# Weight sums of the first fifteen seven-product projections: from GpSimd to VectorE, in another order

## The chip, the core and the metric

One core of a Trainium2 chip runs the whole program once. The time is the device time of one execution in microseconds. Before the change three executions took 2179.86, 2184.01 and 2181.0 us, a median of 2181.0 us.

## What is computed

The reference is one step of a one-layer encoder over 1024 prompt tokens and 64 sample tokens of width 1024, all in float32. Cut to what this change touches, it is a normalised input times one large weight matrix:

```python
rq, rk, rv, rg, sq, sk, sv, ga, gb = split(rms_norm(x, g_attn) @ w_in)
q, k, v = rope(rq), rope(rk) / 16, rv                  # 4 heads of 256
o, state = retention(q, k, v)                          # chunkwise, chunks of 64
B = sliding_window_attention(sq, sk, sv)               # 16 query heads, 2 key/value heads of 64
```

Gates, output projections, cross-attention and a SwiGLU block follow; nothing of them is changed.

## The kernel before, in words

Activations lie transposed: features on the 128 partitions, the 1088 tokens along the free axis, cut into two halves of 544. Every float32 operand is kept as a rounded high part and a remainder, and each product is three matmuls (high by high, high by low, low by high).

Most projections take 256 output columns at a time and are 2 by 2 block products: two weight rows of blocks by two column halves, times two feature halves by two token halves. `strassen` (L254) computes them with seven products in place of eight, in the order P1, P2, P6, P5, P7, P3, P4. One product is 24 matmuls of 272 columns and fills one PSUM pair of banks; three pairs are in turn. The operands on the activation side (B11, B21, T1 to T4 and so on) are made once. The weight side is made anew for every projection by `weight_ops` (L173): it takes two raw tiles of 128 by 1024, `raws[0]` with the blocks a11 and a12 and `raws[1]` with a21 and a22, and forms P1 = a11, P2 = a12, P4 = a22, P5 = a21 + a22, P6 = a21 + a22 - a11, P7 = a11 - a21, P3 = a12 - P6. The four sums (L190, L191, L193, L196) are done in place by GpSimd. `put` (L181) sends each result through `split` (L122): ScalarE casts the high part into a `wq` tile (L123), VectorE subtracts to get the low part (L124). There are five `wq` tiles in turn and two raw tiles, so a weight is prepared a few products ahead and waits for a tile that TensorE has left.

VectorE also adds partial products (`u` tiles, L259), takes results out of PSUM (`stage`, L598), applies the rotary terms (L629 to L635; for heads 2 and 3 the last two on GpSimd), adds up squares for the norm (`token_squares`, L478) and does a good part of the retention steps (`retention`, from L740): the low halves of `ks`, `qs`, `st` and `ss`, the scaled keys `kt` (L768) and values `vb` (L777), the masked scores `sf` (L789).

`project_phase` (L572) runs these projections in this order: values of head 0 (eight plain products), then with seven products keys 0, queries 0, keys 1, queries 1, values 1, SWA queries 0, the same four for heads 2 and 3, then the keys and values of SWA together (L686): fifteen projections. After them come the last SWA queries and the gates. Retention steps of the heads are woven in between. After the first queries come the root-mean-square factors: `token_roots` (L480) has TensorE add up the squares over partitions (`pt`, L487).

A scheduler lays down one fixed order per engine before the program runs, and each engine then works in that order. So an instruction that moves from GpSimd to VectorE also moves its neighbours, on TensorE too.

Of the kernel before, what the change touches and what calls it, by code (L numbers as in the profile page):

```python
# [109 lines left out]
class Kernel:  # L110
# [62 lines left out]
    def weight_ops(self, raws, n=512, skip=()):  # L173

        nc = self.nc
        half = [[raws[i][:, j * n:(j + 1) * n] for j in range(2)] for i in range(2)]
        (a11, a12), (a21, a22) = half
        add, sub = ALU.add, ALU.subtract
        w = {}

        def put(name, src):  # L181
            if name in skip:
                return
            q = w[name] = self.new_op({"P7": 2, "P6": -1, "P5": -1}.get(name, 0))
            self.split(src, q[:, 0, :n], q[:, 1, :n])

        tt = nc.gpsimd.tensor_tensor
        put("P1", a11)
        put("P2", a12)
        tt(out=a11, in0=a11, in1=a21, op=sub)  # L190
        tt(out=a21, in0=a21, in1=a22, op=add)  # L191
        put("P7", a11)
        tt(out=a11, in0=a22, in1=a11, op=sub)  # L193
        put("P6", a11)
        put("P5", a21)
        tt(out=a12, in0=a12, in1=a11, op=sub)  # L196
        put("P3", a12)
        put("P4", a22)
        return w
# [153 lines left out]
    def run(self):  # L353
        nc, tc, io = self.nc, self.tc, self.io
        with ExitStack() as ctx:
            cp = ctx.enter_context(tc.tile_pool(name="const", bufs=1, reuse_waits="tile"))
            self.np = ctx.enter_context(tc.tile_pool(name="norm", bufs=1, reuse_waits="tile"))
            dp = ctx.enter_context(tc.tile_pool(name="scratch", bufs=1, reuse_waits="tile", space=DRAM))

            self.ident = cp.tile([P, P], F32, name="ident")  # L360
            self.ones = cp.tile([P, P], F32, name="ones")
            self.gains = cp.tile([P, 5, KT], F32, name="gains")
            self.load(self.gains, io["g_all"])
            nc.vector.memset(self.ones, 1.0)
            self.rstd = cp.tile([P, T], F32, name="rstd")
            nc.scalar.mul(self.rstd[:, :1], self.ones[:, :1], 1.0)

            self.root = cp.tile([P, len(CH), 3], F32, name="root")
            self.rtok = cp.tile([P, 9], F32, name="rtok")
            nc.vector.memset(self.rtok, 1.0)  # L370
            self.mtok = cp.tile([P, 2], F32, name="mtok")
            self.tab = cp.tile([P, 2, H, 3], F32, name="tab")
            self.tok = cp.tile([P, 3, H, 9], F32, name="tok")
            self.sinks = cp.tile([P, NPAIR], F32, name="sinks")

            self.d_mk = dp.tile([H, P, 2, NMEM], F32, name="d_mk")
            self.d_mv = dp.tile([H, P, 2, NMEM], F32, name="d_mv")
            self.d_ret = dp.tile([KT, P, T], F32, name="d_ret")
            self.d_swa = dp.tile([KT, P, T], F32, name="d_swa")
            self.d_gate = [dp.tile([KT, P, T], F32, name=f"d_gate{i}") for i in range(3)]  # L380
            self.d_mix = dp.tile([KT, P, T], F32, name="d_mix")
            self.d_h = [dp.tile([KT, P, T], F32, name=f"d_h{i}") for i in range(2)]
            self.d_op = dp.tile([len(OPS), FT // 2, P, HALF], F32, name="d_op")
            self.d_rb = dp.tile([16, 64 * 256], F32, name="d_rb")

            self.d_qkv = dp.tile([3, KT, P, T], F32, name="d_qkv")
            self.d_skv = dp.tile([2, P, T], F32, name="d_skv")
            self.d_sq = dp.tile([NPAIR // 2, P, 17, 2, 64], F32, name="d_sq")

            with ExitStack() as sctx:  # L390
                self.rings = [Ring(sctx.enter_context(tc.tile_pool(name=f"ring{i}", bufs=1, reuse_waits="tile", side="right")))
                              for i in range(2)]
                self.mem = sctx.enter_context(ExitStack())
                self.left = sctx.enter_context(ExitStack())
                self.sixth, self.turns, self.held, self.last_held = None, 0, [], 0
                self.wp = self.left.enter_context(tc.tile_pool(name="weights", bufs=2, reuse_waits="tile"))
                self.project_phase()
                with self.plain_psum(2, side="right"):
                    self.swa_phase()
                with self.plain_psum(side="right"):  # L400
                    self.merge_swa()
                    self.mem.close()
                    self.cross_phase()
                rp = sctx.enter_context(tc.tile_pool(name="rf", bufs=1, reuse_waits="tile", side="right"))
                self.rstd_f = rp.tile([P, T], F32, name="rstd_f")
                self.temp = sctx.enter_context(ExitStack())
                self.new_b12(self.temp, side="right")
                self.cross_out_phase()
                self.ffn_phase()
# [162 lines left out]
    def project_phase(self):  # L572
        nc, tc, io = self.nc, self.tc, self.io
        with ExitStack() as ctx:
# [89 lines left out]
            with ExitStack() as rctx:  # L664
                self.ra = rctx.enter_context(tc.tile_pool(name="ra", bufs=1, reuse_waits="tile"))
                rope = self.ra.tile([P, 2, T], F32, name="rope")
                for t in range(2):
                    self.load(rope[:, :, half(t)], io["c_rope"][:, :, half(t)])
                for h in range(H):
                    rotated(pair("w_k", h) if h else first, h, 1)  # L670
                    if h == 0:
                        self.token_squares()
                    rotated(pair("w_q", h), h, 0)
                    if h == 0:
                        self.token_roots()
                        self.retention_setup()
                    else:
                        values(pair("w_v", h), h)
                    if h:
                        project(pair("w_sq", h - 1), queries(h - 1))  # L680
                    self.retention(h)
                    if h == 0:
                        self.spread_roots()
                    if h == 1:
                        self.later.append(self.bias_table)
                project(self.load_ops((io["w_sk"], io["w_sv"])), lambda i, t, o: self.store(self.d_skv[i, :, half(t)], o))  # L686
            project(pair("w_sq", 3), queries(3))
            steps = [0, 0, 0, 0, 1, 2, 2, 3, 3, 3, 2, 0]
            for idx, w, act in ((1, "w_ga", AF.Sigmoid), (0, "w_rg", AF.Silu), (2, "w_gb", AF.Sigmoid)):
# [1144 lines left out]
```

## Time and profile before

| | |
|---|---|
| Runs, median | 2181.0 us |
| The profiled execution: its time, its span | 2183.19 us, 2181.1 us |
| TensorE matmul busy | 2142.3 us, 98% |
| VectorE busy | 1553.4 us, 71% |
| ScalarE busy | 876.4 us, 40% |
| GpSimd busy | 651.7 us, 30% |
| Mean granted TensorE clock | 0.995 |
| First sum (L190) of the fifteen projections, first sum of the next one | 40.18 us, 462.81 us |

The span goes from the first to the last instruction; 2.1 us of the execution's time lie around it. Matmuls are pipelined, so "busy" says that TensorE has something under way and not that it works at its peak; what stops it is read from the waits. The changed stretch is about 36 to 462 us.

### The profile page before, as it was taken

What the parts mean: (1) busy time and instruction counts of PE and PEld (TensorE: products, weight loads), DVE (VectorE), ACT (ScalarE), POOL (GpSimd) and SP (SyncE); (2) the same over time, 40 slices, a digit from 0 to 9 for tenths busy, and PEclk for the clock granted to TensorE, in tenths of its full rate; (3) what the DMA queues carried; (4) which work ended last, traced back from release to release, by engine and by line L of the source; (5) the groups of instructions that cost most, each with busy time, mean ns of one, the idle gap of its engine ahead of it and who ended that gap; (6) DMA issues with size and microseconds to landing.
All of it is one profiled execution on the core that took longest, in us unless ns stands there. A gap on an engine that the chain in (4) does not pass through costs nothing. (4 is left out here: it accounts for less than half of the span.)

```text
span 2181.1 us, 41848 instructions
## 1 busy us (share of the span) xinstructions
PE 2142.3 (98%) x16389; PEld 2089.0 (96%) x16389; DVE 1553.4 (71%) x2824; ACT 876.4 (40%) x1898; POOL 651.7 (30%) x498
## 2 busy tenths in 40 slices
PE   8999999999999999999999999999999999999997
PEld 8999999999999997889999999999999999999997
DVE  8996868776687658665455555768777777787688
ACT  7344424344344447553233333333322322344343
POOL 1223233342344214430000000014565555514531
PEclk9999999999999999999999999999999999999999
DMA  6434354435344467326443111422333323294433
GB/s 208 154 131 114 114 152 125 137 111 159 103 160 164 166 206 246 118 80 219 124 155 120 40 49 59 146 87 91 121 124 116 105 96 120 94 331 128 135 107 119
DMA packets 181446, 290.84 MB, mean 133 GB/s; under 512 B 40290, under 2 KB 109314, under 8 KB 181250
## 3 DMA queue, kind: packets, MB, share of 16 engines
q1 hardware_dynamic: 176130, 278.18, 40.1%
q10 hardware_dynamic: 4608, 8.36, 1.0%
q8 instruction: 129, 2.11, 0.4%
q0 software_dynamic: 512, 1.64, 0.2%
q14 instruction: 67, 0.55, 0.1%
HBM read 196.95 MB, written 91.16 MB: 132 GB/s over the span
## 5 line engine op out<-in xcount | busy, mean ns | idle before, releaser
L124 DVE TENSOR_TENSOR wq<-raw,wq 128x512 fp32r<-128x512 f32 (+1 forms) x499 | 443.9, 893 | 134.8 <-ACT wq L123 131.4
L123 ACT CAST wq<-raw 128x512 fp32r<-128x512 f32 (+1 forms) x499 | 303.1, 614 | 567.1 <-PE pq L215 223.3
L212 PE MATMUL pq<-T,wq 128*128 128x272 f32 x1832 | 492.0, 288 | 4.9 <-ACT wq L123 3.3
L213 PE MATMUL pq<-T,wq 128*128 128x272 f32 x1832 | 492.9, 289 | 0.0
L213 PE MATMUL pq<-B,wq 128*128 128x272 f32 x1592 | 428.2, 289 | 2.9 <-DVE B L124 2.6
L212 PE MATMUL pq<-B,wq 128*128 128x272 f32 x1592 | 426.6, 288 | 0.5 <-ACT B L123 0.5
L190 POOL TENSOR_TENSOR raw<-raw 128x512 f32<-128x512 f32 (+1 forms) x59 | 86.0, 1458 | 1036.5 <-DVE rs_r L301 483.0
L215 PE MATMUL pq<-T,wq 128*128 128x272 f32 x1832 | 382.8, 289 | 1.5 <-DVE wq L124 1.5
L212 PEld LDWEIGHTS pq<-T,wq 128*128 128x128 f32 x1832 | 345.0, 188 | 6.7 <-ACT wq L123 3.1
L213 PEld LDWEIGHTS pq<-T,wq 128*128 128x128 f32 x1832 | 344.9, 188 | 1.2 <-issue 1.1
L215 PE MATMUL pq<-B,wq 128*128 128x272 f32 x1592 | 332.2, 289 | 0.0
L213 PEld LDWEIGHTS pq<-B,wq 128*128 128x128 f32 x1592 | 299.5, 188 | 4.3 <-DVE B L124 4.2
L212 PEld LDWEIGHTS pq<-B,wq 128*128 128x128 f32 x1592 | 299.4, 188 | 1.4 <-ACT B L123 0.9
L215 PEld LDWEIGHTS pq<-T,wq 128*128 128x128 f32 x1832 | 290.2, 190 | 2.6 <-DVE wq L124 1.8
L215 PEld LDWEIGHTS pq<-B,wq 128*128 128x128 f32 x1592 | 252.2, 190 | 0.5 <-issue 0.4
L259 DVE TENSOR_TENSOR u<-pq,u 128x544 f32<-128x544 f32 x177 | 127.2, 719 | 95.5 <-PE pq L215 95.4
L193 POOL TENSOR_TENSOR raw<-raw 128x512 f32<-128x512 f32 (+1 forms) x59 | 80.8, 1370 | 91.4 <-DVE wq L124 81.5
L598 DVE TENSOR_TENSOR stage<-pq,u 128x544 f32<-128x544 f32 x112 | 80.3, 717 | 36.9 <-PE pq L215 32.4
L191 POOL TENSOR_TENSOR raw<-raw 128x512 f32<-128x512 f32 (+1 forms) x59 | 88.8, 1505 | 3.6
L196 POOL TENSOR_TENSOR raw<-raw 128x512 f32<-128x512 f32 (+1 forms) x59 | 84.0, 1423 | 4.4
L1483 POOL TENSOR_TENSOR stage<-stage,rstd_f 128x544 f32<-128x544 f32 x40 | 63.9, 1607 | 39.1 <-ACT stage L1482 39.1
L156 PE MATMUL pd<-xc,wq 128*128 128x256 f32 (+1 forms) x256 | 74.5, 291 | 0.0
(383 smaller groups left out, 4548.4 us busy)
## 6 DMA issues: line engine op xcount, KB each, us to landing
hl<-d_op SPq DMA_DIRECT2D x85, 272.0 KB, 5.3
d_qkv<-stage SPq DMA_DIRECT2D x44, 272.0 KB, 2.7
d_op<-stage SPq DMA_DIRECT2D x44, 272.0 KB, 2.1
d_op<-ht SPq DMA_DIRECT2D x44, 272.0 KB, 3.3
raw<-w_gate SPq DMA_DIRECT2D x22, 512.0 KB, 3.6
raw<-w_up SPq DMA_DIRECT2D x22, 512.0 KB, 4.0
raw<-w_down SPq DMA_DIRECT2D x16, 512.0 KB, 4.8
d_gate<-stage ACTq DMA_DIRECT2D x28, 272.0 KB, 3.0
```

The source lines that it names most:

```text
L123: self.last_cast = self.nc.scalar.copy(hi, src).ins
L124: return self.nc.vector.tensor_tensor(out=lo, in0=src, in1=hi.bitcast(F32), op=ALU.subtract).ins
L156: mm(ps, wh, xh, start=start, stop=False)
L190: tt(out=a11, in0=a11, in1=a21, op=sub)
L191: tt(out=a21, in0=a21, in1=a22, op=add)
L193: tt(out=a11, in0=a22, in1=a11, op=sub)
L196: tt(out=a12, in0=a12, in1=a11, op=sub)
L212: mm(ps[:, c, :HC], w[:, 0, ks], x[:, 0, cs], start=start, stop=False)
L213: mm(ps[:, c, :HC], w[:, 0, ks], x[:, 1, cs], start=False, stop=False)
L215: self.last_mm = mm(ps[:, c, :HC], w[:, 1, ks], x[:, 0, c * HC:(c + 1) * HC], start=False, stop=stop).ins
L259: add = lambda out, a, b: nc.vector.tensor_tensor(out=out, in0=a, in1=b, op=ALU.add)
L598: nc.vector.tensor_tensor(out=o, in0=ps, in1=sb, op=ALU.add)
```

## The change

For the fifteen projections from the first keys to the keys and values of SWA, the four sums are done by VectorE (`self.sums_by = nc.vector`), and in another order: a21 + a22 comes first and right behind P1, then P6 = that sum minus a11, and P7 = a22 - P6 last. Before, a11 - a21 came first, and P6 was the third sum in the chain. P7 is also prepared behind P6 and P5 now, in the order in which the products use them, and so takes its `wq` tile in plain turn. All later projections keep GpSimd and the old order.

```diff
+            q = w[name] = self.new_op(0 if self.sums_by is nc.vector else {"P7": 2, "P6": -1, "P5": -1}.get(name, 0))
...
+        tt = self.sums_by.tensor_tensor
         put("P1", a11)
+        if self.sums_by is nc.vector:
+            tt(out=a21, in0=a21, in1=a22, op=add)
+            put("P2", a12)
+            tt(out=a11, in0=a21, in1=a11, op=sub)
+            put("P6", a11)
+            put("P5", a21)
+            tt(out=a12, in0=a12, in1=a11, op=sub)
+            tt(out=a11, in0=a22, in1=a11, op=sub)
+            put("P7", a11)
+        else:
...
         put("P3", a12)
         put("P4", a22)
...
+                self.sums_by = nc.vector
                 self.project_phase()
...
+            self.sums_by = nc.gpsimd
             project(pair("w_sq", 3), queries(3))
```

The order of the engines' instructions changes at many places between the first keys and the SWA keys and values, and hardly behind them. Three places matter below. Line numbers of the changed kernel are 10 to 12 higher from `strassen` on.

VectorE at the first keys, before (`raw_521` is `raws[0]`, `raw_523` is `raws[1]`; `wq_525` and `wq_528` are P1 and P2, `wq_533` is P7, `wq_537` is P6, `wq_540` is P5; the T tiles are activation operands):

```order
L124 TENSOR_TENSOR wq_525<-raw_521,wq_525 128x512
L124 TENSOR_TENSOR wq_528<-raw_521,wq_528 128x512
L124 TENSOR_TENSOR T4_303<-xg2_143,T4_303 128x544 x2
L124 TENSOR_TENSOR T3_250<-xg1_142,T3_250 128x544
L124 TENSOR_TENSOR wq_533<-raw_521,wq_533 128x512
L124 TENSOR_TENSOR T4_304<-xg3_144,T4_304 128x544 x2
L598 TENSOR_TENSOR stage0_552<-pq_590,u1_560 128x544
L124 TENSOR_TENSOR wq_537<-raw_521,wq_537 128x512
L124 TENSOR_TENSOR wq_540<-raw_523,wq_540 128x512
```

The same place after (`wq_533` is P6 now, `wq_536` is P5):

```order
L124 TENSOR_TENSOR wq_525<-raw_521,wq_525 128x512
L124 TENSOR_TENSOR wq_529<-raw_521,wq_529 128x512
L124 TENSOR_TENSOR T4_303<-xg2_143,T4_303 128x544
L190 TENSOR_TENSOR raw_523<-raw_523 128x512
L124 TENSOR_TENSOR T4_303<-xg2_143,T4_303 128x544
L124 TENSOR_TENSOR T3_250<-xg1_142,T3_250 128x544
L192 TENSOR_TENSOR raw_521<-raw_523,raw_521 128x512
L195 TENSOR_TENSOR raw_521<-raw_521 128x512
L124 TENSOR_TENSOR T4_304<-xg3_144,T4_304 128x544 x2
L124 TENSOR_TENSOR wq_533<-raw_521,wq_533 128x512
L609 TENSOR_TENSOR stage0_552<-pq_590,u1_560 128x544
L124 TENSOR_TENSOR wq_536<-raw_523,wq_536 128x512
```

Three sums now stand among the T operands, and P6's low part has moved ahead of the result of P2 (`stage0_552`).

TensorE where the second half of the tokens' squares is added up (`pt_1057`), before: in the first product of keys 1 (`pq_1640`), with one of its 24 matmuls left.

```order
L213 MATMUL pq_1640<-B11_187,wq_1611 128x272
L215 MATMUL pq_1640<-B11_187,wq_1611 128x272
L487 MATMUL pt_1057<-ones_64,rstd_68 128x2 x4
L487 MATMUL pt_1057<-ones_64,rstd_68 64x2
L215 MATMUL pq_1640<-B11_187,wq_1611 128x272
```

After: behind the whole second product and four matmuls each of P6 (`pq_1698`) and P5 (`pq_1724`).

```order
L222 MATMUL pq_1724<-T1_188,wq_1622 128x272
L223 MATMUL pq_1724<-T1_188,wq_1622 128x272
L498 MATMUL pt_1057<-ones_64,rstd_68 128x2 x4
L498 MATMUL pt_1057<-ones_64,rstd_68 64x2
L225 MATMUL pq_1698<-T2_247,wq_1619 128x272 x2
```

So `pt` stands 1 + 24 + 4 + 4 = 33 matmuls later on TensorE.

VectorE around the third retention block of head 0 (`ks_1313`, `st_1292`, `kt_1324`), before:

```order
L634 TENSOR_TENSOR stage0_552<-stage0_552,stage1_553 128x544
L630 TENSOR_TENSOR stage1_553<-stage1_553,rope_557 128x544
L124 TENSOR_TENSOR ks_1313<-ks_1313 128x512
L124 TENSOR_TENSOR st_1292<-state_1166,st_1292 128x512
L861 TENSOR_TENSOR rv_1296<-rv_1296,tok_75 128x2
```

After, where the block's steps stand behind the first weights of the next projection (`raw_2297`, `raw_2299`):

```order
L190 TENSOR_TENSOR raw_2299<-raw_2299 128x512
L192 TENSOR_TENSOR raw_2297<-raw_2299,raw_2297 128x512
L195 TENSOR_TENSOR raw_2297<-raw_2297 128x512
L124 TENSOR_TENSOR wq_2309<-raw_2297,wq_2309 128x512
L196 TENSOR_TENSOR raw_2297<-raw_2299,raw_2297 128x512
L124 TENSOR_TENSOR ks_1313<-ks_1313 128x512
L609 TENSOR_TENSOR stage0_552<-pq_2243,u5_2109 128x544
L124 TENSOR_TENSOR st_1292<-state_1166,st_1292 128x512
```

All four sums of a projection stand nearly together ahead of the block's steps, and the block has moved about a projection later.

More of the change, by code (lines that the diff above doesn't have):

```diff
@@ L183, in put @@
                 return
-            q = w[name] = self.new_op({"P7": 2, "P6": -1, "P5": -1}.get(name, 0))
+            q = w[name] = self.new_op(0 if self.sums_by is nc.vector else {"P7": 2, "P6": -1, "P5": -1}.get(name, 0))
             self.split(src, q[:, 0, :n], q[:, 1, :n])
-        tt = nc.gpsimd.tensor_tensor
+        tt = self.sums_by.tensor_tensor
         put("P1", a11)
[L189 to L196, printed above, removed]
+        if self.sums_by is nc.vector:
[8 more added lines that the diff above has]
+        else:
+            put("P2", a12)
+            tt(out=a11, in0=a11, in1=a21, op=sub)
+            tt(out=a21, in0=a21, in1=a22, op=add)
+            put("P7", a11)
+            tt(out=a11, in0=a22, in1=a11, op=sub)
+            put("P6", a11)
+            put("P5", a21)
+            tt(out=a12, in0=a12, in1=a11, op=sub)
         put("P3", a12)
```

## Prediction

> **What bounds the kernel now.** I read the page's first part, then TensorE's waits in the changed stretch, then the granted clock around the two longest, then the engines at those places.
>
> ```profile
> PE 2142.3 (98%) x16389; PEld 2089.0 (96%) x16389; DVE 1553.4 (71%) x2824; ACT 876.4 (40%) x1898; POOL 651.7 (30%) x498
> ```
>
> TensorE has a matmul under way 98% of the time, and weight loads run 96%. The change removes no matmul. It can win only time in which TensorE stands still or runs slowly in the changed stretch, so the waits there are the whole prize (engine, line and what was waited for; then total us, times, longest):
>
> ```profile
> PE pb L870 <- ACT ret_o L864: 2.5, 3, 1.4
> PE pq L212 <- ACT wq L123: 2.4, 1, 2.4
> PE pss L156 <- DVE kt L768: 2.3, 2, 1.4
> PE pt L487 <- DVE rstd L478: 2.0, 1, 2.0
> PE pq L212 <- DVE u L259: 1.6, 1, 1.6
> PE pq L215 <- DVE wq L124: 0.5, 1, 0.5
> ```
>
> Together they make 11.3 us. One is for a weight's high part, one for a low part; the others are for work that VectorE does or passes on. Two of them also cost clock (stretch: its length, busy time and matmuls, PEclk, DMA share, GB/s):
>
> ```profile
> 46.09:49.50 3.41, 1.36 (x10) 1.00 1.03 387
> 49.50:52.92 3.42, 3.42 (x18) 0.50 0.45 141
> 52.92:56.33 3.41, 3.41 (x29) 1.00 0.89 296
> 93.88:97.29 3.41, 2.57 (x21) 1.00 0.00 0
> 97.29:100.70 3.41, 3.41 (x18) 0.50 0.00 0
> ```
>
> The clock was 0.50 for 3.41 us right behind each of the waits at 45.7 and 92.7 us. Such a stretch starts 18 matmuls where a full one starts 29: 11 fewer, at 0.125 us each (24 matmuls of a product in 3.0 us, as the rows of TensorE below have them) 1.4 us. So the prize is at most 11.3 + 2 x 1.4 = 14.1 us.
>
> **The first P6 (gain).** The 2.4 us wait is at the first keys. The rows are of the timeline: start, length, engine, what, and in brackets the idle time before.
>
> ```profile
> 39.42 1.28 DVE L124 TENSOR_TENSOR wq<-raw,wq 128x512 fp32r<-128x512 f32 x2
> 40.62 1.99 DVE L124 TENSOR_TENSOR T<-xg,T 128x544 fp32r<-128x544 f32 x3
> 40.18 3.58 POOL L190 TENSOR_TENSOR raw<-raw 128x512 f32<-128x512 f32 x1 [39.73 <-DVE wq L124]
> 43.84 1.29 POOL L191 TENSOR_TENSOR raw<-raw 128x512 f32<-128x512 f32 x1
> 45.76 1.68 POOL L193 TENSOR_TENSOR raw<-raw 128x512 f32<-128x512 f32 x1 [0.63 <-DVE wq L124]
> 44.45 1.23 DVE L124 TENSOR_TENSOR wq<-raw,wq 128x512 fp32r<-128x512 f32 x1 [1.84 <-ACT wq L123]
> 45.41 0.60 ACT L262 COPY u<-pq 128x544 f32<-128x544 f32 x1
> 47.47 1.14 ACT L123 CAST wq<-raw 128x512 fp32r<-128x512 f32 x2 [1.45 <-POOL raw L193]
> 45.30 0.41 PE L215 MATMUL pq<-B,wq 128*128 128x272 f32 x2
> 48.14 0.39 PE L212 MATMUL pq<-T,wq 128*128 128x272 f32 x1 [2.42 <-ACT wq L123]
> ```
>
> P2 ends at about 45.55. P6 needs three sums of GpSimd in a chain, which run from 40.18 to 47.44, and a cast; TensorE starts P6 at 48.14. After the change I walk VectorE's new order with durations from these rows: two low parts take 1.20 from start to the next start, so one 128x512 operation costs 0.60; three T operands take 1.99, so 0.64 each. Both raw tiles are in SBUF by 40.18, since GpSimd read both then. From 40.62: T4 to 41.26, a21 + a22 to 41.86, T4 and T3 to 43.14, P6's sum to 43.74, P3's to 44.34. ScalarE now has the copy of P1's result, two T4 casts and then P6's cast. P1 ends 24 matmuls ahead of 45.55, at 42.55; copy to 43.2, T4 casts (two in 1.14, as in the row of the casts) to 44.3, P6 high to 44.9, in time. VectorE does the T4 low parts from 44.34 to 45.62 and P6's low part to 46.25, while TensorE asks for it after four matmuls, at 46.05. So 0.2 us of the 2.42 stay: minus 2.2. No wait, no half clock behind it: minus 1.4. The first term is **-3.6 us**. If the T casts came up to 0.5 us late it would be -3.1.
>
> **The price on VectorE.** Fifteen projections of four sums are 60 new operations. No row shows VectorE doing this sum; the nearest is the low part of the same 128x512 shape, also with two SBUF inputs, at 0.60: 36 us. From below they could cost nothing where VectorE waits anyway, from above 0.68, the whole length, 41 us. Against it stands what GpSimd's sums now cost VectorE. This is the start, 36 to 110 us, where GpSimd does sums alone (count, busy us, mean ns):
>
> ```profile
> L124 DVE TENSOR_TENSOR wq<-raw,wq 128x512 fp32r<-128x512 f32 x22 | 16.5, 759 | 2.4 <-ACT wq L123 2.4
> L478 DVE TENSOR_TENSOR rstd<-rstd,xsq 128x544 f32<-128x544 f32 x14 | 11.5, 827 | 0.2
> L124 DVE TENSOR_TENSOR T<-xg,T 128x544 fp32r<-128x544 f32 x9 | 7.1, 832 | 0.0
> L629 DVE TENSOR_TENSOR stage<-stage,rope 128x544 f32<-128x544 f32 x5 | 5.8, 1151 | 0.0
> L631 DVE TENSOR_TENSOR stage<-stage,rope 128x544 f32<-128x544 f32 x5 | 4.6, 930 | 0.0
> L632 DVE TENSOR_TENSOR stage<-stage,rope 128x544 f32<-128x544 f32 x4 | 4.0, 990 | 0.0
> L630 DVE TENSOR_TENSOR stage<-stage,rope 128x544 f32<-128x544 f32 x4 | 3.9, 986 | 0.0
> L635 DVE TENSOR_TENSOR stage<-stage 128x544 f32<-128x544 f32 x4 | 2.8, 710 | 0.0
> ```
>
> An undisturbed operation of 544 columns takes 710 ns (last row), one of 512 columns 680. Over that, the seven rows hold 1.7 + 1.6 + 1.1 + 2.2 + 1.1 + 1.1 + 1.1 = 9.9 us. That is the time in which an operation with two SBUF inputs stands behind a GpSimd sum. The sums of the first three projections add 12 x 0.60 = 7.2 us there. VectorE gets 2.7 us **lighter** at the start. For the whole stretch (the last two rows are sums over it, of all engines and of GpSimd's sums alone):
>
> ```profile
> L124 DVE TENSOR_TENSOR wq<-raw,wq 128x512 fp32r<-128x512 f32 x106 | 85.0, 804 | 21.5 <-ACT wq L123 21.3
> L630 DVE TENSOR_TENSOR stage<-stage,rope 128x544 f32<-128x544 f32 x16 | 17.2, 1078 | 0.0
> L124 DVE TENSOR_TENSOR ks<-ks 128x512 fp32r<-128x512 f32 x14 | 15.1, 1079 | 3.6 <-PE pk L736 3.6
> L632 DVE TENSOR_TENSOR stage<-stage,rope 128x544 f32<-128x544 f32 x16 | 14.4, 901 | 0.1
> sum 426.00, PE 414.60 PEld 404.99 DVE 343.08 ACT 171.60 POOL 138.12; mean PE 27.64 PEld 27.00 DVE 22.87 ACT 11.44 POOL 9.21
> sum 426.00, POOL 91.95; mean POOL 11.49
> ```
>
> The first four rows hold 13.1 + 5.9 + 5.6 + 3.0 = 27.6 us of such delay; the sums are 91.95 of GpSimd's 138.12 us, two thirds, so 18 us go with them. VectorE ends up 36 - 18 = 18 us heavier at most in 426 us, of which it is now idle 426 - 343 = 83. That fits; but it no longer helps behind the start.
>
> **Queries 0 (gain).** Two waits, 0.5 for a low part and 1.6 for a partial sum, fall at 73 and 80 us, where VectorE never rests:
>
> ```profile
> 78.77 0.71 DVE L635 TENSOR_TENSOR stage<-stage 128x544 f32<-128x544 f32 x1
> 79.40 0.71 DVE L259 TENSOR_TENSOR u<-pq,u 128x544 f32<-128x544 f32 x1
> 60.00:84.00 24.00, 23.42 (x33) 1.00 0.54 173
> ```
>
> The partial sum that frees TensorE's bank stands behind rope work. TensorE comes 3.6 us earlier here, but VectorE also loses its 1.84 us wait for P7's cast (row at 44.45) and 2.7 us of work. I take both waits as gone: **-2.1 us**, between -2.1 and 0.
>
> **The factors `pt` (nothing).** On TensorE `pt` stands 33 matmuls, 4.1 us, later. VectorE has 13 more operations ahead of the last square, 10 of them sums: 13 x 0.62 = 8.1 us more, less 9.9. It was ready at 94.66, so now at 92.9; TensorE, then at 92.7, comes at 92.7 - 3.6 - 2.1 + 4.1 = 91.1. The wait stays near 2 us with its half clock: **0**, between -3.4 (both go) and +1.
>
> **Retention (nothing).** Waits for `kt` and `ret_o`, 4.8 us, end in chains that pass VectorE several times. Some shorten with the contention, others have sums in front now. I take **0**, between -4.8 and the rival's +9.6 below.
>
> DMA and ScalarE get nothing new; raw tiles are asked for a little earlier or later, as their last reader moves. GpSimd's other work only gains room. Behind 462 us the order is nearly the same and TensorE still bounds, so what is won stays won. The sum is -3.6 - 2.1 = -5.7 us against the profiled execution's own 2183.2 us, of which 2181.1 is the span: 2177.5. That execution lies 2.2 us over the median of the three runs, 2181.0, and so against the median I expect 2175.3, rounded to **2175**.
>
> **Rules beside rows.** The Trainium skill, "Perfetto Trace Analysis", section "Optimizing Scalar/DVE Operations", says that where the vector engine is saturated, moving work off it, even to GpSimd, may make sense; it adds that the two share a read port, so that it might not help. The first half speaks against this change, since VectorE is at 23.42 of 24 us; the contention rows bear the second half out. "TensorE: Matmul & The Clock Gate", section "HAM oscillation", gives idle gaps over about 3.4 us as what costs clock; here 2.42 us did. By it the -1.4 would not come.
>
> **Rivals.** *All goes:* the contention was behind the retention waits too, and `pt` is met in time. The prize of 14.1 less what is counted: 2167 to 2171. For it: 18 us of delays vanish. Against: the sums' 36 us.
>
> *Given back:* VectorE's saturation decides. It rests 0.58 of the 24 us from 60 to 84, in which TensorE does about one projection. If no delay vanishes, four sums of 0.60 leave it 1.8 us late for each projection there; queries 0, keys 1 and queries 1 make 5.5 us, which eat the 5.7: 2181. For it: TensorE already waits twice there. Against: the 9.9 us of delays that go.
>
> *Slower:* VectorE's fixed order. Four sums, 2.4 us, stand nearly together ahead of `ks` and `st` of a retention block, which TensorE waits for in its own order. There are 15 such chains for heads 0 to 2. Five waits now cost 4.8 us, 0.96 each; if every chain met one, 14.4, so 9.6 more, and queries 0 would gain nothing. 9.6 - 3.6 = +6.0: 2187. It decides once eight more chains wait. Against it: retention was moved later on TensorE too.
>
> *Clock:* half-clock stretches come whatever happens at the first P6: -2.2 - 2.1, or 2176.7.
>
> **How the numbers follow.** The forecast has 0.45, with its own range 2171 to 2179; all goes 0.15; given back 0.20; slower 0.15; clock 0.05. Two tenths of a percent, 4.4 us, is about what a measurement of this kernel can tell from no change, so faster means under 2176.6. Of the forecast three quarters lie there (0.33), with 0.15 and 0.02 from all goes and clock: 0.50. Slower, over 2185.4, is the slower rival and a tail of the third: 0.17. The rest, 0.33, is same. The range goes from all goes to slower, 2167 to 2187.
>
> **What would show it.** At the first keys the idle time ahead of the first P6 matmul falls from 2.42 to under 0.5 us, and no 0.50 clock follows. `wq` low parts come near 680 ns on the mean of 36 to 110 us, and sums of raw tiles on VectorE near 0.60 us apart. The `u` wait at queries 0 goes. If TensorE's waits for `kt`, `ks` or `ret_o` sum to over 8 us more than 4.8, the slower rival holds; if its waits for `u` and `stage` grow between 60 and 134 us, saturation does. The forecast is wrong from the root if P6 still waits at the first keys.

## The result, and the profile after

| | before | after |
|---|---|---|
| Median of 17 executions each, side by side | 2181.86 us | 2178.61 us |
| Lowest and highest | 2177.62, 2187.99 | 2174.18, 2181.84 |
| Ratio, with 95% interval | | 0.9978, 0.997 to 0.9986 |
| Profiled execution, its span | 2183.19, 2181.1 | 2174.66, 2172.7 |

The change made the kernel 0.22% faster. By that ratio it is 4.8 us, and the two medians lie 3.3 us apart, hardly over what the measurement can tell. The two profiled executions lie 8.5 us apart, more than the ratio says: the one after is the fourth lowest of its 17, the one before lies 1.3 us over its median. The section on the changed kernel run again comes back to that.

The first part of the page after:

```profile
PE 2140.9 (99%) x16389; PEld 2088.6 (96%) x16389; DVE 1555.6 (72%) x2884; ACT 876.0 (40%) x1898; POOL 559.1 (26%) x438
```

Sixty operations went from GpSimd (498 to 438) to VectorE (2824 to 2884). VectorE's busy time over the whole program grew by 2.2 us only. TensorE's waits in the changed stretch, 36 to 462 us, after:

```profile
PE po L156 <- DVE ret_t L884: 1.4, 2, 1.2
PE pq L222 <- ACT wq L123: 0.7, 1, 0.7
PE pq L225 <- DVE wq L124: 0.6, 1, 0.6
PE po L156 <- ACT ss L123: 0.6, 1, 0.6
PE po L158 <- DVE ss L124: 0.6, 1, 0.6
PE pss L156 <- DVE rr L311: 0.3, 1, 0.3
```

They make 4.2 us where they made 11.3. The waits for the first P6, for `u`, for `pt`, `kt` and `ret_o` are all gone. The row of 36 to 108 us before (busy us and instructions of PE, PEld, DVE, ACT, POOL, then PEclk, DMA share, GB/s) holds the rest:

```profile
36.00:108.00 72.00, 65.42 (x496) 64.64 (x495) 67.21 (x100) 30.73 (x54) 21.08 (x12) 0.95 0.53 177
```

And after:

```profile
36.00:108.00 72.00, 72.00 (x579) 71.94 (x579) 69.64 (x130) 31.96 (x56) 0.00 (x0) 1.00 0.55 186
```

TensorE starts 83 more matmuls in the same 72 us. At 0.125 us each that is 10.4 us. It never stands still, and no half clock is left.

To see where time is won or lost later I set the start of the n-th matmul on TensorE beside that of the n-th matmul before. This is the difference in us for the changed kernel and the experiments below. Inside the stretch the n-th matmul need not be the same one, but the amount of work done is nearly the same. The last column is a control with the order of before.

| n (time before) | after | again | after, cut | vector, old order | the same, cut | GpSimd, new order | the same, cut | first 3 | the same, cut | other 12 | control, cut |
|---|---|---|---|---|---|---|---|---|---|---|---|
| 300 (48.1) | -2.9 | -2.9 | -2.7 | 0.2 | 0.1 | -2.6 | -3.0 | -2.4 | -2.6 | 0.1 | -1.0 |
| 480 (72.1) | -4.5 | -4.5 | -4.3 | 0.2 | -1.4 | -0.8 | -2.0 | -4.1 | -4.2 | 0.0 | -1.0 |
| 600 (89.6) | -7.0 | -7.1 | -6.9 | -1.7 | -2.3 | -1.2 | -1.4 | -6.6 | -6.8 | 0.0 | -1.0 |
| 660 (100.9) | -10.9 | -11.0 | -10.7 | -5.6 | -6.2 | -4.6 | -5.1 | -10.5 | -10.6 | 0.2 | -3.7 |
| 900 (130.5) | -8.8 | -9.4 | -8.3 | -5.3 | -5.0 | -2.8 | -3.6 | -6.0 | -6.7 | 0.3 | -3.7 |
| 2400 (323.1) | -11.7 | -12.7 | -11.3 | -8.2 | -7.8 | -2.3 | -2.9 | -6.5 | -6.2 | 0.7 | -2.9 |
| 2700 (360.7) | -9.3 | -10.3 | -8.8 | -1.2 | -6.7 | 1.5 | -4.0 | -0.1 | -7.1 | 7.4 | -4.0 |
| 4140 (543.9) | -10.0 | -11.0 | -9.4 | -3.0 | -8.5 | 1.6 | -4.0 | -0.4 | -6.6 | 5.9 | -3.3 |
| 6300 (812.0) | -9.6 | -11.6 | -9.9 | -3.6 | -9.0 | 1.0 | -4.6 | -0.9 | -6.7 | 5.4 | -3.7 |
| 6700 (872.2) | -9.1 | -6.6 | -3.0 | -5.7 | -9.0 | 4.7 | 0.0 | 1.0 | -3.3 | 3.3 | -3.2 |
| 16300 (2158.4) | -8.3 | -8.1 | -1.5 | -0.3 | -6.8 | 6.7 | -1.3 | 1.9 | -3.3 | 4.9 | -2.4 |

In the column "after" all is won by matmul 660, about 100 us in. Of the 10.9 us, 0.3 were there at matmul 250, ahead of the changed stretch. From 660 to 4140 the rest of the stretch gives back 0.9 us, and the rest of the kernel 1.7 us. The waits of the stretch fell by 7.1 us and two half clocks went, 2.8 us by the prediction's count. Together that is 9.9 us, and 10.0 us are won at matmul 4140: the waits account for the gain of this execution.

### The profile page after: what moved, and what is told of

Same layout as the page of the kernel before. It is cut to its first block, busy times and chain, and to the rows that moved or that the text cites. A ratio compares the mean times of both kernels' runs of the same rounds, so it can differ in the third digit from the quotient of the medians.

```text
span 2172.7 us, 41775 instructions
## 1 busy us (share of the span) xinstructions
PE 2140.9 (99%) x16389; PEld 2088.6 (96%) x16389; DVE 1555.6 (72%) x2884; ACT 876.0 (40%) x1898; POOL 559.1 (26%) x438
## 4 chain that ended last, share of the span: by engine, by line
PE 72%; DVE 4%; DMA 2%; issue 2%; ACT 1%; POOL 1%; SPq 0%; POOLq 0%; DVEq 0%; ACTq 0%
PE pq L225 14%; PE pq L222 14%; PE pq L223 14%; PE pd L156 8%; PE pd L158 8%; PE pd L157 8%; PE pss L984 1%; PE pout L1047 1%; DVE wq L124 1%; PE pp L1023 1%; DMA ld<-d_swa 0%; DVE y L1577 0%; PE css L157 0%; PE css L156 0%; PE css L158 0%
## 5 line engine op out<-in xcount | busy, mean ns | idle before, releaser
L200 POOL TENSOR_TENSOR raw<-raw 128x512 f32<-128x512 f32 (+1 forms) x44 | 63.4, 1442 | 829.1 <-DVE rs_r L311 483.5
L615 POOL TENSOR_TENSOR stage<-stage,rstd 128x544 f32<-128x544 f32 x20 | 32.2, 1616 | 341.3 <-ACT rstd L510 216.6
L156 PE MATMUL pd<-xc,wq 128*128 128x256 f32 (+1 forms) x256 | 74.5, 291 | 0.0
L158 PE MATMUL pd<-xc,wq 128*128 128x256 f32 (+1 forms) x256 | 74.1, 289 | 0.0
L157 PE MATMUL pd<-xc,wq 128*128 128x256 f32 (+1 forms) x256 | 73.7, 288 | 0.0
```

The source lines that it names most:

```text
L156: mm(ps, wh, xh, start=start, stop=False)
L157: mm(ps, wh, xl, start=False, stop=False)
L158: self.last_mm = mm(ps, wl, xh, start=False, stop=stop).ins
```

## The experiments

| label | what it is | median, before beside it | ratio, 95% interval |
|---|---|---|---|
| e1_order_pool | new order, sums on GpSimd | 2188.28, 2182.09 | 1.0033, 1.002 to 1.0045 |
| e2_vec_oldorder | sums on VectorE, old order | 2180.94, 2182.09 | 0.9995, 0.9985 to 1.0006 |
| e3_first3_vec | the change in the first 3 projections | 2186.2, 2182.09 | 1.0014, 1.0004 to 1.0024 |
| e4_rest_vec | the change in the other 12 | 2189.16, 2182.09 | 1.0034, 1.0021 to 1.0046 |
| e5_first3_small | first 3, store cut to 64 KB | 2180.02, 2180.77 | 0.9998, 0.9988 to 1.0007 |
| e6_before_small | before, store cut | 2182.9, 2180.77 | 1.0007, 0.9997 to 1.0017 |
| e7_first3_head0 | first 3, table one head earlier | 2183.3, 2180.77 | 1.0008, 0.9998 to 1.0018 |
| e8_after_head0 | after, table one head earlier | 2183.59, 2180.77 | 1.0012, 1.0004 to 1.0021 |
| e9_after_small | after, store cut | 2179.28, 2181.43 | 0.9994, 0.9984 to 1.0004 |
| e10_vec_old_small | VectorE, old order, store cut | 2177.26, 2181.43 | 0.9984, 0.9973 to 0.9994 |
| e11_order_pool_small | GpSimd, new order, store cut | 2186.65, 2181.43 | 1.0023, 1.0012 to 1.0034 |
| e12_after_again | after, not altered | 2177.21, 2181.43 | 0.9987, 0.9976 to 0.9998 |

e1 and e4 are medians of 5 executions each, the others of 11 or 12.

### Engine and order apart, and the projections apart

Four edits of the changed kernel, in which the order (with the turn of the `wq` tiles) and the engine are chosen by a count of the projections. Each line of the four stands alone in its run; the two lines that set `self.sums_by` go:

```diff
+        self.calls = n_call = getattr(self, "calls", 0) + 1
+        first_sum, by_vector = n_call <= 15, False                  # e1_order_pool
+        first_sum, by_vector = False, n_call <= 15                  # e2_vec_oldorder
+        first_sum, by_vector = n_call <= 3, n_call <= 3             # e3_first3_vec
+        first_sum, by_vector = 3 < n_call <= 15, 3 < n_call <= 15   # e4_rest_vec
...
-            q = w[name] = self.new_op(0 if self.sums_by is nc.vector else {"P7": 2, "P6": -1, "P5": -1}.get(name, 0))
+            q = w[name] = self.new_op(0 if first_sum else {"P7": 2, "P6": -1, "P5": -1}.get(name, 0))
...
-        tt = self.sums_by.tensor_tensor
+        tt = (nc.vector if by_vector else nc.gpsimd).tensor_tensor
...
-        if self.sums_by is nc.vector:
+        if first_sum:
```

> The new order of the sums (a21 + a22 first, P6 second, P7 last) for the same fifteen projections, but still on GpSimd. Theory (the order frees the first P6, VectorE's relief frees queries 0 and the factors): TensorE's wait at the first P6 falls from 2.4 us to under 1 and its half clock goes, the waits at queries 0 and at pt stay within 1 us of 2.1 and 2.0, and the time falls by 3 to 4 us. Rival (only the faster engine matters): the first P6 still waits over 1.5 us and the time stays within 1.5 us of before.

> The sums of the fifteen projections on VectorE, but in the old order (a11 - a21 first, P6 behind the third sum). Theory: P6's sum now stands behind the result of P2 on VectorE, so the first P6 waits 1.5 to 2.5 us as before, with half clock; with GpSimd silent the waits at queries 0 and pt shrink to under 1 us together, and the time falls by 4 to 6 us. Rival (the order is the whole gain): nothing or less than 1.5 us is won.

> Only the first three projections (keys 0, queries 0, keys 1) have their sums on VectorE in the new order; the other twelve stay on GpSimd in the old order. Theory (the gain is the start): the same point of TensorE's work at about 100 us comes 10 to 11 us earlier than before, as in the changed kernel, and the time is within 2 us of the changed kernel's. Rival (every projection wins its share): a fifth of the gain, 1 to 2 us.

> The other twelve projections on VectorE in the new order, the first three on GpSimd in the old one. Theory: the waits at the first P6 and at queries 0 stay as before, what follows is a wash, and the time is within 2 us of before. Rival (every projection wins its share): four fifths of the gain, 4 us or more.

None of the four is faster than before by what can be told, and three are a little slower, so all four times miss what was expected. At the start the traces are clearer. The new order alone takes the first P6's wait away: -2.6 by matmul 300. The engine alone doesn't. These are TensorE's waits at the start of VectorE in the old order, and the clock around the first:

```profile
PE pq L226 <- ACT wq L123: 3.0, 1, 3.0
PE pq L226 <- DVE u L273: 0.4, 1, 0.4
```

```profile
46.25:49.66 3.41, 1.32 (x10) 1.32 (x11) 3.41 (x6) 2.54 (x5) 0.00 (x0) 1.00 1.06 395
49.66:53.07 3.41, 3.41 (x17) 3.41 (x17) 3.31 (x6) 2.39 (x5) 0.00 (x0) 0.50 0.63 204
```

In the old order P6's sum is still the third one, so TensorE waits 3.0 us for it even with VectorE, and 3.41 us at half clock follow. The engine alone takes away most of the `u` wait instead. The order alone still has a `u` wait of 1.7 us and gets a new one of 1.6 us for `xsq` near 68 us; of the 3.5 us that it had won at matmul 400, 0.8 are left at 480. Either one alone takes the `pt` wait away, and wins there, from 600 to 660, what both together win (3.4 and 3.9 us; both 3.9). So the parts don't add up. By matmul 600, ahead of `pt`, the order has won 1.2 us, the engine 1.7 and both together 7.0: P6 needs the order, and what follows needs the engine. The first three projections alone have it all (-10.5 by matmul 660), the other twelve none of it (0.2).

All four then lose 4 to 7 us between matmuls 2400 and 2700 (2.4 us in the changed kernel). In the run with the first three projections that is one wait of TensorE:

```profile
PE pss L156 <- DVE kt L782: 5.8, 1, 5.8
```

Its DMA queue on SP (SyncE) there (start, us, issues):

```profile
304.23 0.35 SPq L117 DMA_DIRECT2D raw<-w_k  x1
305.00 0.36 SPq L120 DMA_DIRECT2D d_ret<-ret_t  x1
305.92 0.67 SPq L120 DMA_DIRECT2D d_rb<-rb  x1
308.22 0.35 SPq L117 DMA_DIRECT2D raw<-w_k  x1
```

And its DMA issues from 300 to 345 us (count, KB each, us to landing; of the two weight loads only the one behind the store has a landing in the trace):

```profile
raw<-w_k SPq DMA_DIRECT2D x2, 512.0 KB, 13.3
d_rb<-rb SPq DMA_DIRECT2D x1, 1024.0 KB, 13.0
```

`d_rb` is the table of the attention bias. `bias_table` (in the retention blocks of head 1) stores it to memory 32 times over, 1 MB in one store. It takes some 13 us to land, and a weight tile issued 2.3 us behind it lands late as well. GpSimd waits for that tile:

```profile
321.64 1.28 POOL L204 TENSOR_TENSOR raw<-raw 128x512 f32<-128x512 f32 x1 [12.22 <-DMA raw<-w_k]
```

Before, the next weight loads are issued 15 us behind the store (300.77, then 316.24) and take 5.2 us. In the changed kernel the load near it is issued 1.4 us ahead (325.81, then 327.23) and takes 3.6. In e1 two loads, 2.0 and 5.5 us behind the store, take 12.1 and 11.2 us; in e2 two, 2.2 and 10.5 us behind it, take 13.1 and 6.8. In e4 it is likely the stores behind it (`d_sq<-stage`, 6.6 us against 2.9 after); no run tested that. So between these matmuls, where the scheduler lays this one store decides more than the edit under test.

### The store cut

To test that, the store was cut to 64 KB, with every other instruction in the same order. These kernels leave out 30 of the 32 repeats, and the attention reads its bias from one repeat, which is not the right one, so only their times are of use:

```diff
-        self.store(self.d_rb.rearrange("h (i c) -> h i c", c=512),
-                   rb.rearrange("p a b -> p (a b)").unsqueeze(1).broadcast_to([16, 32, 512]))
+        self.store(self.d_rb.rearrange("h (i c) -> h i c", c=512)[:, :2],
+                   rb.rearrange("p a b -> p (a b)").unsqueeze(1).broadcast_to([16, 2, 512]))
...
-                src = self.d_rb.rearrange("(p e) c -> e c p", e=2)[e, 63:63 + 64 * 255, :]
-                src = src.rearrange("(i c) p -> i p c", c=255)[:, :, :NKEY]
+                src = self.d_rb.rearrange("(p e) c -> e c p", e=2)[e, 63:63 + 255, :]
+                src = src.rearrange("(i c) p -> i p c", c=255)[:, :, :NKEY].broadcast_to([64, NPAIR, NKEY])
```

> The kernel with the first three projections on VectorE, with the store of the bias table cut from 1 MB to 64 KB (2 of the 32 repeats; the bias is later read from one repeat). Every engine's order of instructions stays; the attention bias is not the right one. Theory (the loads of the next weights stand behind that store): the weights of keys 2 land within 6 us of their issue instead of 13, TensorE's wait of 5.8 us for kt near 334 us falls under 1 us, and the time is 5 to 7 us under that of the kernel with the first three projections. Rival (VectorE's or GpSimd's order is at fault there): the wait stays over 4 us and the time within 1.5 us of that kernel's.

> The kernel before with the same cut of the bias table's store, a control. In it no weight load is issued within 10 us behind the store, so theory expects no change: within 2 us of before. Rival (the store's traffic slows every kernel): 4 us or more under before.

With the store cut, the DMA issues of the first three projections in the same window read:

```profile
raw<-w_k SPq DMA_DIRECT2D x2, 512.0 KB, 3.6
raw<-w_q SPq DMA_DIRECT2D x2, 512.0 KB, 3.5
d_rb<-rb SPq DMA_DIRECT2D x1, 64.0 KB, 2.6
```

The 5.8 us wait for `kt` falls to 0.6. Between matmuls 2400 and 2700 the run wins 0.9 us where it lost 6.4, and its median lies 6.2 us under that of the uncut kernel (beside medians of before that differ by 1.3; by the ratios it is 3.5 us). Cut in the kernel before, where no weight load stands close behind it, the store brings nothing: 1.0007. So this loss was the store's. But at 0.9998 the first three projections are still not shown to have the changed kernel's gain (0.9978) in their runs: from matmul 660 to 900 this trace gives back 3.9 us, with a wait of 2.8 us for `vb` near 112 us, where the changed kernel gives back 2.1.

The control shows one more thing, in TensorE's waits:

```profile
PE pt L487 <- DVE rstd L478: 0.8, 1, 0.8
```

The order of all work there is that of before, yet the `pt` wait is 0.8 us, not 2.0, and no half clock follows it. By matmul 660 this execution is 3.7 us ahead of before's profiled one, 0.9 of it from ahead of the changed stretch and 2.7 from `pt`. In e4, whose TensorE has the order of before up to 117 us, the wait is 2.3 us, with a half clock. So executions of one and the same order differ here, and before's profiled execution was one of the costly ones. Beside the control, the changed kernel would win 1.2 us at `pt` in place of 3.9.

### The store earlier

Can the store be moved where it harms nobody? `bias_table` was put one head earlier (`if h == 1:` became `if h == 0:`), in the first-three kernel and in the changed one.

> The kernel with the first three projections on VectorE, with the whole bias table made and stored one head earlier, where both weight loads of the next projection stand ahead of the store in the queue. Theory: the 5.8 us wait near 334 us goes and none of its size comes in its place; 4 to 6 us under before. Rival (the start's gain is lost on the way whatever the store does): within 2 us of before or slower.

> The changed kernel with the bias table made one head earlier; weight loads stand behind three stores behind it. Theory: the changed kernel had nothing to lose to the store at its old place, so nothing to win: 3 to 7 us under before, like the changed kernel. Rival (the store cost the changed kernel too): 9 us or more under before.

The wait near 334 us goes in the first-three kernel, but others come, and at 1.0008 it is not the 4 to 6 us under before that were expected. TensorE's new wait there, then the new one in the changed kernel:

```profile
PE pk L750 <- DMA ks<-d_qkv: 3.3, 1, 3.3
```

```profile
PE pkv L156 <- DVE vb L789: 5.2, 1, 5.2
```

In the latter VectorE stands ahead of it, held by a store that stands in the queue behind the table:

```profile
236.88 0.72 DVE L609 TENSOR_TENSOR stage<-pq,u 128x544 f32<-128x544 f32 x1 [6.37 <-DMA d_sq<-stage]
```

From matmul 1500 to 1800 the first loses 7.5 us, the second 10.3. The collision was only moved, to 213 and 222 us. In the changed kernel, whose store harmed nobody, the move cost more than the whole change had won: 1.0012, where as fast as the changed kernel was expected.

### Order by engine, without the store

The same cut, in the changed kernel and in e2 and e1:

> The changed kernel with the bias table's store cut from 32 repeats to 2 (1 MB to 64 KB); the attention reads its bias from one repeat, which is not the right one, so only the time is of use. Every engine's order of work is otherwise that of the changed kernel. Theory (the store hurts only where weight or retention loads stand behind it within some 5 us; in the changed kernel the one load near it is issued 1.4 us ahead of it): as the changed kernel, 3 to 7 us under before, ratio 0.997 to 0.9985. Rival (the changed kernel too pays for its store, unseen): some 4 us lower still, ratio about 0.995 to 0.9965.

> The sums on VectorE in the order of before, with the store cut to 64 KB (the bias is read from one repeat, not the right one). Theory (the 7 us lost between matmuls 2400 and 2700 are the store's): those come back, 5 to 8 us under before, ratio 0.9965 to 0.9977: the engine alone then gives about what the whole change gives, the order of the sums about nothing, since the first wait for P6 goes but others come late. Rival (the engine alone gives nothing, the new order is what counts): as the uncut kernel, ratio 0.999 to 1.0005.

> The new order with the sums still on GpSimd, with the store cut to 64 KB (the bias is read from one repeat, not the right one). Theory: the 4 us lost between matmuls 2400 and 2700 come back and the rest stays, about 3 us over before, ratio 1.000 to 1.002: the order alone gives nothing. Rival (the loss is in GpSimd's sums under the new order, not in the store): as the uncut kernel, 1.002 to 1.0045.

In both traces that had the loss, it is gone: from 2400 to 2700 VectorE in the old order now loses 1.1 us (7.0 uncut), GpSimd in the new order wins 1.1 (3.9 lost). Their ratios fell by 0.0011 and 0.0010, some 2.3 us each, less than the traces show (the profiled execution of e11 was the lowest of its twelve) and short of what was expected of e10 and e11. The changed kernel with the store cut came out at 0.9994, above what was expected, though the intervals overlap. In its trace the cut changed nothing for TensorE near the store, as the theory has it (from 2400 to 2700 it loses 2.5 us, 2.4 uncut), though a load of `vf` 6.9 us behind the store landed in 3.1 us in place of 6.8. It stands at -9.9 at matmul 6300 and at -3.0 at matmul 6700.

From GpSimd to VectorE the ratio falls in the new order by 0.0055 (0.0029 with the store cut) and in the old order by 0.0005 (0.0023). From the old order to the new one it rises on GpSimd by 0.0033 (0.0016) and on VectorE goes from 0.9995 to 0.9978 uncut, and from 0.9984 to 0.9994 cut. So the engine's side is the better one in all four comparisons (in the old order uncut by less than can be told), and the order by itself is worth nothing that can be shown, although the start needs it; the next section shows a place where it costs. Where the 5 us go by which the runs of e11 still lie over before is open. None of these kernels is shown to be faster than the changed one.

### The changed kernel again

> The changed kernel once more, not altered. Theory: ratio 0.997 to 0.9986 again, the executions again in two groups some 4 us apart (near 2175 and near 2180). If this profile falls in the upper group, the steps against matmul numbers show where the 4 us are: by theory in the entry of the sliding-window attention (809 to 850 us), with a second half-clock stretch there. Rival: they are at the start, a wait with its half clock that comes back in some executions.

The ratio was 0.9987, so the gain is there again. It is smaller by the ratio, but the medians lie 4.2 us apart here, and the two intervals overlap. Twelve executions were 2175.0 to 2177.6 nine times and 2180.1 to 2181.4 three times. In the first series eight lay from 2174.2 to 2175.5 and nine from 2178.6 to 2181.8. The profiled one fell in the lower group both times. But the two traces differ at the entry of the sliding-window attention. This is TensorE's longest wait from 795 to 860 us in the first profile, and then in the second:

```profile
PE pd L156 <- ACT swin L963: 2.2, 1, 2.2
```

```profile
PE pd L156 <- ACT swin L963: 5.0, 1, 5.0
```

TensorE waits for a copy by ScalarE, which stands behind casts of gate tiles that are just being loaded. The first profile's timeline of ScalarE:

```profile
832.68 0.91 ACT L123 CAST ret<-swin 128x320 fp32r<-128x320 f32 x2 [0.95 <-DMA swin<-d_gate]
834.26 0.94 ACT L123 CAST ret<-swin 128x320 fp32r<-128x320 f32 x2 [0.67 <-DMA swin<-d_gate]
...
836.15 0.26 ACT L963 COPY swin<-pd 128x128 f32<-128x128 f32 x1
```

The second profile's:

```profile
832.15 0.99 ACT L123 CAST ret<-swin 128x320 fp32r<-128x320 f32 x2 [3.26 <-DMA swin<-d_gate]
834.24 0.90 ACT L123 CAST ret<-swin 128x320 fp32r<-128x320 f32 x2 [1.10 <-DMA swin<-d_gate]
...
836.09 0.26 ACT L963 COPY swin<-pd 128x128 f32<-128x128 f32 x1
```

TensorE started matmul 6500 at 834.0 us in the first and at 831.1 us in the second, but the copy came at 836.1 in both. The loads set that time, so what TensorE had won was given back. Behind the longer wait there was half a clock as well; the windows of the first profile, then of the second:

```profile
835.20:842.00 6.80, 5.54 (x36) 5.07 (x37) 5.68 (x26) 5.45 (x21) 1.76 (x3) 1.00 0.95 270
```

```profile
835.20:842.00 6.80, 5.61 (x20) 4.85 (x20) 3.76 (x16) 3.66 (x14) 1.75 (x3) 0.50 0.98 287
```

From matmul 6300 to 6700 the step is +0.5 us in one execution of the changed kernel, +5.0 in the other, and +6.9 in the kernel with the store cut, whose order is the same but for that store. In VectorE with the old order and the store cut it is nothing. The expectation was a profile from the upper group, and there was none. The second execution has the long wait and is still the lowest of its twelve, so this entry alone does not make the two groups. What makes them is open.

The gate loads come late for a reason that came with the change. GpSimd issues four stores here, `d_mv` and `o_mv` twice each. The first store of each pair and the operation behind them, in GpSimd's rows of the timeline before:

```profile
820.51 0.58 POOL L1168 DMA_DIRECT2D d_mv<-swin  x1 [0.97 <-ACT swin L1167]
...
821.62 0.54 POOL L1168 DMA_DIRECT2D d_mv<-swin  x1
...
824.96 0.91 POOL L994 TENSOR_TENSOR t<-t,den 128x256 f32<-128x256 f32 x1 [2.26 <-DVE den L992]
```

After, the second pair stands behind that operation:

```profile
808.68 0.58 POOL L1180 DMA_DIRECT2D d_mv<-swin  x1 [1.43 <-ACT swin L1179]
...
812.66 0.91 POOL L1006 TENSOR_TENSOR t<-t,den 128x256 f32<-128x256 f32 x1 [2.86 <-DVE den L1004]
813.53 0.58 POOL L1180 DMA_DIRECT2D d_mv<-swin  x1
```

A gate load in SP's queue then waits for one of these stores (SP's waits after, 816 to 838 us):

```profile
SPq L117 <- DMA o_mv<-swin: 5.3, 1, 5.3
```

In all nine traces with the new order in the first three projections the second pair stands behind, SP waits 4.4 to 5.9 us for a store of `o_mv`, and TensorE waits 1.3 to 5.0 us for the copy. In all five with the old order there the four stores stand together, SP does not wait for them, and TensorE waits 0.2 us. From matmul 6300 to 6700 the nine give back 0.5 to 6.9 us, the five at most 0.5. So behind the changed stretch the order is not quite the same, and the difference costs. No run puts the stores back, so that they cause the wait is read from the traces and not tested; why the scheduler moved them is not known.

## Why the prediction was right, point by point

It said 2175.0 us against a median of 2181.0, a ratio of 0.9972. Measured were 0.9978 and, in the second series, 0.9987. The mechanism was right; one term was much too small, and one sentence of the sum did not hold. These two errors have opposite signs. By matmul 660 the trace had won 10.9 us where 5.7 were forecast, while the runs show 4.8 and 2.8. So that the time came out near is in part luck, and 2178.61 us is close to the upper end of the forecast's own range.

**The first P6: right.** The walk along VectorE had a21 + a22 start at 41.26 and P6's sum end at 43.74; the timeline after, VectorE's rows and ScalarE's:

```profile
40.84 0.68 DVE L190 TENSOR_TENSOR raw<-raw 128x512 f32<-128x512 f32 x1
42.71 0.68 DVE L192 TENSOR_TENSOR raw<-raw 128x512 f32<-128x512 f32 x1
44.51 1.14 ACT L123 CAST wq<-raw 128x512 fp32r<-128x512 f32 x2
45.38 0.68 DVE L124 TENSOR_TENSOR wq<-raw,wq 128x512 fp32r<-128x512 f32 x1
```

P6's sum ends at 43.39, its low part at 46.06 (46.25 was forecast), no wait is left and the clock stays whole from 46 us. By matmul 480 4.5 us are won (0.3 of them ahead of the stretch), where 3.6 were forecast. That a wait of 2.42 us cost clock is mostly borne out: a half clock also stood behind this wait in e4 and e6 (2.3 us each) and in e2 (3.0 us), but not in e10 (2.9 us), and it went with the wait here. By the Trainium skill, "TensorE: Matmul & The Clock Gate", section "HAM oscillation", with its gaps of over about 3.4 us, none of these waits would have had one; the measurement decides against it.

**The price on VectorE: right, but set far too high.** For nearly the same work, from 36 us to the first sum of the next projection (462.81 us before, 452.79 after), VectorE was busy as follows, before and then after:

```profile
36.00:462.80 426.80, 415.40 (x3277) 405.79 (x3276) 343.84 (x619) 172.07 (x377) 138.12 (x89) 0.99 0.45 137
```

```profile
36.00:452.80 416.80, 412.52 (x3274) 402.33 (x3274) 347.30 (x680) 172.21 (x377) 45.61 (x30) 1.00 0.46 139
```

That is 3.5 us more, where at most 18 were forecast. Sixty sums of 684 ns are 41 us, so VectorE's other operations took some 37 us less; the prediction took 18 off for delays behind GpSimd, from four groups of rows alone. At the start, 36 to 110 us, the delays behind GpSimd are gone (count, busy us, mean ns):

```profile
L124 DVE TENSOR_TENSOR wq<-raw,wq 128x512 fp32r<-128x512 f32 x23 | 15.1, 683 | 0.5 <-ACT wq L123 0.5
L489 DVE TENSOR_TENSOR rstd<-rstd,xsq 128x544 f32<-128x544 f32 x14 | 10.1, 719 | 0.5 <-ACT xsq L487 0.5
L190 DVE TENSOR_TENSOR raw<-raw 128x512 f32<-128x512 f32 x4 | 2.7, 684 | 0.0
```

The means were 759 and 827 before. The sums take 684 ns, and 0.60 us from start to the next start (40.84 to 41.44 us, for one), as forecast.

**Queries 0: right.** From matmul 480 to 600 2.5 us are won, 2.1 were forecast.

**The factors `pt`: wrong.** Nothing was forecast, -3.4 at the best. From matmul 600 to 660 3.9 us are won. The last square was to end at 92.9 and TensorE to come at 91.1. In the trace after, VectorE's row and TensorE's:

```profile
87.17 0.72 DVE L489 TENSOR_TENSOR rstd<-rstd,xsq 128x544 f32<-128x544 f32 x1
```

```profile
89.67 1.16 PE L498 MATMUL pt<-ones,rstd 128*128 128x2 f32 x10
```

The square ends at 87.89, 5.0 us ahead of the forecast. The step that failed is "10 of them sums: 13 x 0.62 = 8.1 us more, less 9.9". It counts VectorE's operations and their delays, but not the time in which VectorE itself stood still. That is the length less DVE's busy time in these two rows, of before up to its last square, and of after up to `pt`:

```profile
36.00:94.66 58.66, 52.14 (x401) 51.39 (x399) 54.08 (x71) 26.13 (x45) 21.08 (x12) 0.97 0.55 185
```

```profile
36.00:89.60 53.60, 53.60 (x431) 53.58 (x431) 53.02 (x85) 27.39 (x46) 0.00 (x0) 1.00 0.59 199
```

It was 4.58 us before and 0.58 after (none of that behind the square). These 4.0 us, taken off 92.9, give 88.9, ahead of TensorE at 89.7. Before, it had been waiting for casts of weights (2.4 us in the prediction's row of `wq`, 1.84 of them for P7's) and for TensorE:

```profile
L259 DVE TENSOR_TENSOR u<-pq,u 128x544 f32<-128x544 f32 x6 | 4.3, 717 | 2.0 <-PE pq L215 2.0
```

The same change made both earlier. The prediction took the first into account for queries 0 and forgot both here. And the prize was in part a matter of the execution: the control, with nothing changed at this place, wins 2.7 of the 3.9 us.

**Retention: nearly right.** The old waits of 4.8 us went, but new waits of 1.3 us came at 112 to 116 us for weights of the next projection, and others behind them; the net from matmul 660 to 4140 is +0.9 us. The slower rival, a wait in each chain, did not come: VectorE keeps the time for the sums.

**"What is won stays won": wrong in its place.** It rested on the order being nearly the same behind 462 us, and there two of GpSimd's stores had moved. In the first profile it cost only 0.5 us at the entry of the sliding-window attention, but 5.0 in the second and 6.9 with the store cut. With the spread of `pt` before, this may be why the runs give 4.8 us and 2.8 us (0.22% and 0.13%) where the two profiles give 8.5. How often either happens is open, since only profiled executions show it.

**Given back, by VectorE's saturation: not seen.** From 36 to 108 us VectorE is busy 69.64 of 72 us and TensorE does not wait. The Trainium skill, "Perfetto Trace Analysis", section "Optimizing Scalar/DVE Operations", grants that moving work off a saturated vector engine may make sense, but adds the shared port. Here the second half counted: a low part takes 759 ns beside GpSimd's sums and 683 without.

## What to carry to other kernels

An operation on GpSimd may cost VectorE as much time, by delaying it, as the operation would take there; put the delays and VectorE's own idle time into the sum before calling it saturated. Two halves of a change can need each other: test each alone, and don't expect their gains to add up. A gain at the start of a program is kept only up to the next place where a transfer sets the time, so look for loads that land just in time along the whole program, and compare the order there too, far behind the place of the edit. And before an experiment with a scheduler that reorders everything is believed, see which large store its new order has put ahead of a load.

## What the runs showed of the hardware that was not expected

A store of 1 MB that repeats a small tile took 12.7 to 13.3 us to land. 512 KB loads issued 2.0 to 2.3 us behind it on the same queue took 12.1 to 13.3 us, one 5.5 us behind it 11.2. With the store cut to 64 KB the same loads took 3.6 to 4.2. While the store ran, about 100 GB/s were moved, against up to 398 while a weight tile was still landing (first three projections with the table one head earlier, near 213 us).

Inside the program the granted clock halved in stretches of 3.41 us or twice that. The length of a wait alone did not decide: 3.0 us at the first P6 of e2 cost one such stretch, 2.9 us at the same place in e10, with the same order, none; 2.0 us at `pt` before cost one, 2.2 us at the attention's entry none, 5.0 us there in the other execution two.
